# A one-core hybrid decoder layer: the issue order of all five queues written out by a list scheduler in the source, with fixed numbers of PSUM banks

## Chip, cores and metric

The kernel runs on one core of a Trainium2 chip. The metric is the device time of one execution in microseconds (us), from runs that are not profiled in detail, as a median; a profiled execution beside them gives the views that are read here. Engines: PE is TensorE (PEld its weight loads), DVE is VectorE, ACT is ScalarE, POOL is GpSimd, SP is SyncE, which here only issues DMAs.

## Reference, cut to what matters

One decoder layer on 512 tokens of width 1024, all in fp32:

```python
h = rms_norm(x, pre_g);  proj = h @ w_in          # columns for four head groups and a gate z
o_moba = moba_attention(mq, mk, mv)               # 8 heads x 64; at 512 tokens it is causal attention
o_nsa  = nsa_attention(nq, compressed, selected, window branches, gates)   # 8 heads x 64, 2 kv heads
o_ret  = retention(rq, rk, rv)                    # 4 heads, key 64, value 128, group norm
o_mem  = memory_attention(cq, mem_k, mem_v)       # 4 heads x 128 over 256 memory tokens
y = (concat(o_moba, o_nsa, o_ret, o_mem) * silu(z)) @ w_out
out = x + rms_norm(y, post_g)
```

## The kernel before

**Numbers.** Each fp32 operand is split into a high and a low part of type fp32r (H is a rounded copy, L is the rest), and a product is three matmuls (H·H, H·L, L·H), accumulated in one PSUM bank. The split costs an ACT cast and a subtraction on POOL or DVE for every operand. Weights come in pieces of 128x1024 (512 KB): one DMA on SP into a ring of two raw tiles (`wr`), the ACT cast of L312, the POOL subtraction of L315 into a ring of four (`w`), in `split_to`. All matmuls go through the helper `mm`, line L213; all ring and weight DMAs through `dma`, line L192.

**Two streams.** `g_stream` runs the projections (`dim_job`, `tok_job`: two banks or one of tag G), the norm of the memory, the gates z, and at the end the output projection (`out_job`). `a_stream` runs 28 attention units of four score tiles each (16 NSA, 8 MoBA, 4 memory heads) and then retention (`ret_stream`). The main loop takes a step of one or the other by the ratio of PE time so far (`RATIO`), and that is the program order.

**A unit.** A score tile i: two or three matmuls into a bank S; mask (L961), maximum (L963), reciprocal and gate factor (L921, L923) on DVE; exp (L964) and scaling (L926) on ACT; a 32x32 transpose on DVE into `tb` (L895). When all four are done, `tb` goes by one DMA to DRAM (`pd`) and comes back by four DMAs (`pf`), which completes the transposition. ACT casts it (L914), POOL subtracts (L917), and the tiles `pt` feed the PV matmuls into a bank U (`bU<-pt`). A head's U is emptied by an ACT copy (L987) and a DVE addition (L991). Steps follow each other at lags of one to three score tiles (`LAGS`).

**What sets the order.** The source gives a program order; the compiler's scheduler simulates the machine with its own cost model and orders each engine's queue, with 'keep in program order' edges on some instructions only (`PIN = "hp"`: the first loads, the casts H of L914, the first PV matmul of each step; and nearly all of the start-up, through `pin`). On the chip each queue is executed strictly in that order. PSUM has 8 banks of 128x512 fp32. Tags had up to 5 (S), 2 (T, transposes), 2 (U), 3 (G) and 2 (start-up) buffers, more than 8 in all: the compiler gives out the banks as its schedule has them free.

Of the kernel before, what the change touches and what calls it, by code (L numbers as in the profile page):

```python
# [17 lines left out]
F32 = mybir.dt.float32  # L18
# [6 lines left out]
S = 512  # L25
# [137 lines left out]
LAST_BANK = "U"  # L163
# [6 lines left out]
RATIO = (3.7, 4.39, 2.78, 1.7)  # L170


def hybrid_kernel(ctx, tc, io):
# [100 lines left out]

    def pin(i):

        tc.keep_in_program_order(i)

    state = {"load": 0, "split": 0}

# [515 lines left out]
    def y_evac(t, src, a, b, k):  # L796

        junk = t_([128, 512], F32, "P", PB)
        ACT.activation(junk[:, :b - a], src, AF.Square, accum_out=ssy[:, t, k:k + 1])
        DVE.tensor_tensor(ys[t][:, a:b], src, pg[0][:, a:b], op=ALU.mult)  # L800

    def mean_part(t, ks):

# [4 lines left out]
    def finish(t, k, parts):  # L808
        ACT.activation(ssy[:, t, 3:4], ssy[:, t, k:k + 1], AF.Sqrt, bias=ssy[:, t, 0:1], scale=1.0 / D)
        DVE.reciprocal(ssy[:, t, 3:4], ssy[:, t, 3:4])  # L810
        for a, b in parts:
            y, x = ys[t][:, a:b], xres[t][:, a:b]
            DVE.scalar_tensor_tensor(y, y, ssy[:, t, 3:4], x, op0=ALU.mult, op1=ALU.add)
            nc.sync.dma_start(io["out"][128 * t:128 * t + 128, a:b], y)

    def out_prepare():
        ids = yield from grab(7)
        p = slot(ids[0], [128, 1024], F32)
        nc.sync.dma_start(p, io["post_g"].to_broadcast([128, 1024]))
        pg.append(p)  # L820
        for t in range(4):
            xr = ring("pf", FB, [128, 4, 10, 32], F32).rearrange("p i b c -> p (i b c)")[:, :1024] if t < 2 else slot(ids[3 + t], [128, 1024], F32)
            nc.sync.dma_start(xr, io["x"][128 * t:128 * t + 128, :])
            xres.append(xr)
            ys.append(slot(ids[1 + t], [128, 1024], F32))

# [60 lines left out]
    class Turned:  # L887
# [22 lines left out]
        def split(u, i):  # L910
            n, b = u.blocks(i), u.base(i)
            src = u.near[:, :, b:b + n, :].rearrange("p i k c -> p k i c")
            H, L = [x.rearrange("p k (i c) -> p k i c", i=4) for x in u.place(i)]
            h = ACT.copy(H, src)  # L914
            if "h" in PIN:
                tc.keep_in_program_order(h)
# [11 lines left out]
    class Unit(Turned):  # L928
# [39 lines left out]
        def pv(u, kt):  # L968
            if kt == 0 and u.first:
                u.U[0] = bank("U")  # L970
            U = u.U[0]
            v = vtiles[u.v]
            n = 512 - 128 * kt
            c = 2 * cost(n)
            lastmm = u.last and kt == 3
            for a, pt in enumerate((u.ptH, u.ptL)):
                i = mm(U[:, 128 * kt:512], v[:, u.vh, kt, :], pt[:, 4 * kt:4 * kt + 4 - kt, :],
                   u.first and kt == 0 and a == 0, lastmm and a == 1 and u.cmp_head is None)
                if a == 0 and "p" in PIN:
                    tc.keep_in_program_order(i)  # L980
            if lastmm:
                if u.cmp_head is not None:
                    g = u.cmp_head // 4
                    mm(U, vcz[0][:, u.cmp_head, :], ptc[g][0][:, u.cmp_head % 4 // 2, :], False, True)
                    c += 216
                tmp = t_([64, 512], F32, "P", PB)
                ACT.copy(tmp, U[64:128, :])  # L987
                if u.out not in o_tiles:
                    o_tiles[u.out] = t_([128, 512], F32, "o", 2)
                o = o_tiles[u.out]  # L990
                DVE.tensor_tensor(o[64 * u.half:64 * u.half + 64, :], U[0:64, :], tmp, op=ALU.add)  # L991
                if u.frees:
                    free.extend(u.frees())
            return c
# [6 lines left out]
    class MemUnit(Turned):  # L1001
# [30 lines left out]
        def pv(u, m):  # L1032
# [2 lines left out]
            c = slice(128 * u.h, 128 * u.h + 128)  # L1035
            i = mm(u.U, mv[m][:, 0, c], u.ptH[:, m, :], m == 0, False)
            if "p" in PIN:
                tc.keep_in_program_order(i)
# [380 lines left out]
    plan("NKVC")  # L1419
    plan("NQ0", "CMPK")  # L1420
    plan("NKQ0", "CMPV")
    nc.scalar.dma_start(grow[0].bitcast(F32), io["pre_g"])
    nc.scalar.dma_start(first, io["first"])
# [4 lines left out]
    for t in range(4):  # L1428
# [3 lines left out]
        xx.append(xt)  # L1432
        if t < 2:
            load_to(t)
    nc.sync.dma_start(small, io["small"])
    nc.sync.dma_start(consts, io["consts"])
    mraw = [free.pop(0), free.pop(0)]
    split_to(1)
    wps = bank("S")
# [56 lines left out]
    while streams:  # L1496
# [59 lines left out]
```

## Time and profile before

| what | value |
| --- | --- |
| device time, median of 3 runs | 529.08 us (525.64 to 533.41) |
| the profiled execution's own time | 527.68 us |
| its span, first to last instruction | 525.9 us |
| instructions | 8817 |
| busy: PE, ACT, DVE, POOL | 97%, 68%, 61%, 60% of the span |
| mean granted TensorE clock | 0.992 of 2.4 GHz |

Work outside the span is 527.68 - 525.9 = 1.8 us. A busy PE is not a PE at its peak: a matmul's end is modelled, and the next one overlaps it, so the rate is read from start to start. A wait shorter than that overlap does not show as idle time.

### The profile page before, as it was taken

How to read it: one execution, taken by the hardware profiler on the slowest of the kernel's cores; microseconds unless marked ns; L12 is line 12 of the kernel's file. 1: busy time of each engine (PE TensorE's matmuls, PEld its weight loads, DVE VectorE, ACT ScalarE, POOL GpSimd, SP SyncE). 2: the span in 40 equal slices, each digit the busy share in tenths (PEclk: the TensorE clock that was granted, in tenths of full speed). 3: DMA queues.
4: the chain of work that ended last, by engine and by line, in shares of the span. 5: the costliest groups of instructions: out<-in, count | busy, mean ns of one | idle time of the engine just before them, and what ended most of it. 6: DMA issues, size and time to landing. Idle time of an engine off the chain costs nothing.

```text
span 525.9 us, 8817 instructions
## 1 busy us (share of the span) xinstructions
PE 511.2 (97%) x2854; PEld 444.0 (84%) x2854; DVE 321.7 (61%) x973; ACT 359.9 (68%) x807; POOL 317.5 (60%) x232
## 2 busy tenths in 40 slices
PE   8999999999999999999979999999999999999995
PEld 5988788878888988898858898999899888888884
DVE  6629268766888957757785756359746254652006
ACT  6567689667977889779897977658686474423202
POOL 3165755655876495956766688675566798352600
PEclk9999999999999999999988999999999999999999
DMA  8432437866786795755868868857464464231304
GB/s 309 170 116 95 152 120 219 272 211 221 262 248 227 248 294 164 247 176 176 284 180 251 251 205 288 260 166 248 156 208 154 161 199 129 112 121 43 118 0 160
DMA packets 42335, 100.16 MB, mean 190 GB/s; under 512 B 4529, under 2 KB 21681, under 8 KB 42290
## 3 DMA queue, kind: packets, MB, share of 16 engines
q1 hardware_dynamic: 42144, 99.53, 58.9%
q8 instruction: 22, 0.36, 0.3%
q14 instruction: 23, 0.19, 0.1%
q10 hardware_dynamic: 146, 0.08, 0.1%
HBM read 73.38 MB, written 26.21 MB: 189 GB/s over the span
## 4 chain that ended last, share of the span: by engine, by line
PE 57%; DMA 15%; ACT 12%; POOL 5%; DVE 4%; issue 4%; SPq 2%; ACTq 0%; DVEq 0%; POOLq 0%
PE bG L213 32%; PE bU L213 11%; PE bS L213 10%; DMA pd<-tb 4%; DMA wr<-in_w 4%; POOL w L315 4%; DMA pf<-pd 4%; PE bT L213 3%; ACT w L312 3%; ACT bS L964 2%; SPq L192 2%; ACT pt L914 1%; DMA zd<-R 1%; ACT R L452 1%; ACT bS L926 1%
## 5 line engine op out<-in xcount | busy, mean ns | idle before, releaser
L315 POOL TENSOR_TENSOR w<-wr,w 128x1024 fp32r<-128x1024 f32 x76 | 182.9, 2413 | 99.9 <-ACT w L312 88.5
L213 PE MATMUL bG<-hH,w 128*128 128x512 f32 x576 | 189.8, 397 | 0.2 <-POOL w L315 0.2
L917 POOL TENSOR_TENSOR pt<-pf,pt 128x128 fp32r<-128x128 f32 (+2 forms) x112 | 93.0, 857 | 64.3 <-ACT pt L914 60.0
L213 PEld LDWEIGHTS bG<-hH,w 128*128 128x128 f32 x576 | 108.3, 190 | 22.5 <-POOL w L315 0.8
L213 PE MATMUL bG<-hL,w 128*128 128x512 f32 x288 | 113.5, 394 | 0.0
L312 ACT CAST w<-wr 128x1024 fp32r<-128x1024 f32 x76 | 79.5, 1050 | 49.0 <-DMA wr<-in_w 21.3
L213 PE MATMUL bG<-w,hH 128*128 128x256 f32 (+1 forms) x416 | 82.4, 293 | 0.5 <-DVE R L450 0.4
L213 PEld LDWEIGHTS bG<-w,hH 128*128 128x128 f32 x416 | 66.5, 190 | 2.8 <-PE bG L213 0.9
L895 DVE STREAM_TRANSPOSE tb<-bS 128x128 f32<-128x128 f32 (+2 forms) x112 | 55.4, 500 | 21.9 <-ACT bS L926 21.4
L213 PE MATMUL bS<-R,R 128*128 128x256 f32 (+4 forms) x280 | 61.5, 318 | 2.3 <-DVE tb L895 2.3
L213 PEld LDWEIGHTS bG<-hL,w 128*128 128x128 f32 x288 | 54.6, 190 | 10.2
L213 PE MATMUL bG<-w,hL 128*128 128x256 f32 (+1 forms) x208 | 59.9, 291 | 0.0
L213 PE MATMUL bU<-pt,R 128*128 128x512 f32 (+3 forms) x264 | 56.2, 331 | 3.1 <-DVE o L991 1.2
L914 ACT CAST pt<-pf 128x128 fp32r<-128x128 f32 (+2 forms) x112 | 44.5, 456 | 21.4 <-DMA pf<-pd 18.2
L926 ACT ACTIVATE bS<-bS,st 128x128 f32<-128x128 f32 (+2 forms) x112 | 53.7, 497 | 5.8 <-DVE st L925 2.6
L213 PEld LDWEIGHTS bU<-pt,R 128*128 128x128 f32 x264 | 45.9, 192 | 9.9 <-ACT pt L914 2.5
L213 PEld LDWEIGHTS bS<-R,R 128*128 128x128 f32 x280 | 44.8, 189 | 8.1 <-DVE tb L895 3.0
L964 ACT ACTIVATE bS<-bS,st 128x256 f32<-128x256 f32 (+2 forms) x72 | 40.1, 557 | 10.8 <-DVE st L963 9.2
L213 PEld LDWEIGHTS bG<-w,hL 128*128 128x128 f32 x208 | 39.4, 190 | 0.8
L963 DVE TENSOR_REDUCE st<-bS 128x1 f32<-128x256 f32 (+2 forms) x72 | 38.4, 545 | 0.5
L921 DVE RECIPROCAL st<-st 128x1 f32<-128x1 f32 x112 | 16.6, 154 | 19.3 <-ACT bS L964 16.4
L213 PE MATMUL bG<-w,R 128*128 128x256 f32 (+1 forms) x144 | 24.5, 320 | 0.0
(199 smaller groups left out, 776.6 us busy)
## 6 DMA issues: line engine op xcount, KB each, us to landing
wr<-in_w SPq DMA_DIRECT2D x76, 512.0 KB, 3.7
pd<-tb SPq DMA_DIRECT2D x24, 640.0 KB, 3.6
pf<-pd SPq DMA_DIRECT2D x96, 160.0 KB, 3.6
zd<-R SPq DMA_DIRECT2D x8, 512.0 KB, 4.7
R<-in_mem SPq DMA_DIRECT2D x4, 512.0 KB, 6.4
zb<-zd SPq DMA_DIRECT2D x8, 256.0 KB, 3.7
od<-zb SPq DMA_DIRECT2D x8, 256.0 KB, 4.1
R<-zd SPq DMA_DIRECT2D x4, 512.0 KB, 4.1
```

The source lines that it names most:

```text
L192: i = nc.sync.dma_start(out, a)
L213: return PE.matmul(out, a, b, start=first, stop=last)
L312: h = ACT.copy(H[:, c], w[:, c])
L315: eng.tensor_tensor(L[:, c], w[:, c], H[:, c].bitcast(F32), op=ALU.subtract)
L452: ACT.copy(ks[a][rows[1 - a]], ks[a][rows[a]].bitcast(F32))
L895: DVE.transpose(u.tb[:, :, b:b + n, :].rearrange("p j k c -> p k j c"), p[:, :128 * n].rearrange("p (k j c) -> p k j c", k=n, j=4))
L914: h = ACT.copy(H, src)
L917: POOL.tensor_tensor(L, src, H.bitcast(F32), op=ALU.subtract)
L921: DVE.reciprocal(st[:, 2:3], st[:, 1:2])
L926: ACT.activation(s[:, :w], s[:, :w], AF.Copy, scale=st[:, 2:3])
L963: DVE.tensor_reduce(st[:, 0:1], p[:, :w], axis=AX.X, op=ALU.max, negate=True)
L964: ACT.activation(s[:, :w], p[:, :w], AF.Exp, bias=st[:, 0:1], accum_out=st[:, 1:2])
```

## The change

Every engine call goes through a wrapper (`Engine`) that records the instruction in an `Order`. At the end of the kernel `order.run()` plays the recorded instructions through five in-order queues and one DMA queue with durations and latencies fitted as formulas (`RATES`, `DMA_ISSUE`, `WAIT`), and `order.fix()` chains each engine's instructions in the order that came out, with edges that set the order of issue and add no wait. PE and SP take, of what is ready within 60 ns of the earliest (`PATIENCE`), the first in program order; ACT, DVE and POOL take the one with the earliest due time, worked back from the PE's program order. The other order edges go (`PIN = ""`); the start-up's pins stay, as edges in the recorder. A tile's first write waits for the use of the tile `bufs` before it with its tag, so banks are dealt in program order: S has 4 and now also takes the transposes, U has 1, G has 3. The start-up's two banks are taken from tag U. One DVE multiplication at the very end is pinned. No arithmetic, shape or transfer changes.

```diff
-PS_BUFS = {"S": 5, "T": 2, "U": 2, "G": 3}
-BANKS = {"S": "S", "T": "T", "U": "U", "G": "G", "C": "S"}
+PATIENCE = 60
+DUE = {"PE": 0, "ACT": 1, "DVE": 1, "POOL": 1, "SP": 0}
+DUE_LAG = 300
+WAIT = 45
+DMA_ISSUE = 352
+PS_BUFS = {"S": 4, "U": 1, "G": 3}
+BANKS = {"S": "S", "T": "S", "U": "U", "G": "G", "C": "S"}
-PIN = "hp"
+PIN = ""
...
+class Order:
+    RATES = {"ACT": (170, 0.87), "DVE": (175, 1.02), "POOL": (200, 2.16)}
...
+    def touch(self, op, ap, write):
...
+        inst["w" if write else "r"].append((op["id"], p0, p1, mask))
+        inst["ops"].add(op["id"])
+        if write and inst["old"] is not None:
+            op["pre"] |= inst["old"]["ops"]
+        if inst["prev"] is not None:
+            op["hold"].add(inst["prev"])
+
+    def record(self, name, fn, i, args, kw):
...
+        if "dma" in fn:
+            kb = math.prod(tuple(outs[0].shape)) / 256
+            far = outs[0].space == bass.MemoryType.DRAM
+            small = tuple(outs[0].shape)[0] == 32
+            op["cost"], op["dma"] = DMA_ISSUE, 870 if small else (930 if kb > 200 else 250) + kb * (1.32 if far else 1.47)
+        elif name == "PE":
+            n = math.prod(tuple(outs[0].shape)[1:])
+            op["cost"] = max(108.5, 11 + 0.4246 * n)
+            op["lag"] = op["cost"] + 180
+        else:
+            a, b = self.RATES[name]
+            if fn == "reciprocal" and n > 16:
+                b = 6.3
+            if name == "DVE" and n < 32:
+                a = 140
+            op["lag"] = a + b * n + (190 if kw.get("accum_out") is not None else 0)
+            op["cost"] = op["lag"] - (60 if name == "POOL" else 103 if n >= 32 else 75)
...
+        op["lead"] = op["cost"] + DUE_LAG + (1660 + op["dma"] if "dma" in op else 0)
...
+    def pin(self, i):
+        op = next(o for o in reversed(self.ops) if o["i"] is i)
+        op["hold"] |= {op["prev"]} - {None}
+        return i
+    def run(self):
...
+        due, t = [0.0] * len(ops), 0.0
+        for o in ops:
+            if o["eng"] == "PE":
+                due[o["id"]] = t
+                t += o["cost"]
+            else:
+                due[o["id"]] = math.inf
+        for o in reversed(ops):
+            k = o["id"]
+            for j in after[k]:
+                due[k] = min(due[k], due[j] - (1.0 if k not in ops[j]["pre"] else o["lead"]))
...
+        free = {e: 700.0 for e in avail}
+        line, queue, end = {e: [] for e in avail}, 0.0, 0.0
+        for _ in ops:
+            best = None
+            for e, a in avail.items():
+                if not a:
+                    continue
+                t = max(free[e], min(ready[k] for k in a))
+                k = min((due[k] if DUE[e] else 0, k) for k in a if ready[k] <= t + PATIENCE)[1]
+                t = max(t, ready[k])
+                if best is None or t < best[0]:
+                    best = (t, e, k)
+            t, e, k = best
+            o = ops[k]
+            avail[e].remove(k)
+            line[e].append(k)
+            free[e] = done = t + o["cost"]
+            if "dma" in o:
+                queue = max(queue, done + 1290) + o["dma"]
+                o["fin"] = done = queue + 370
+            else:
+                done = t + o.get("lag", o["cost"])
+            o["t"] = t
+            end = max(end, done)
+            for j in after[k]:
+                p = ops[j]
+                if k not in p["pre"]:
+                    at = t
+                elif p["eng"] == e == "PE":
+                    at = free[e]
+                else:
+                    at = done + WAIT
+                ready[j] = max(ready[j], at)
+                left[j] -= 1
+                if not left[j]:
+                    avail[p["eng"]].append(j)
+        return line, end
+
+    def fix(self):
+        line, end = self.run()
+        for ids in line.values():
+            for a, b in zip(ids, ids[1:]):
+                self.tc.add_manual_dep(self.ops[b]["i"].ins, self.ops[a]["i"].ins.name, mybir.DependencyInfo(
+                    mybir.DependencyClass.NoSync, mybir.DependencyReason.DATA), reason="order of issue")
+        return end
+
...
-    PE, ACT, DVE, POOL = nc.tensor, nc.scalar, nc.vector, nc.gpsimd
+    order = Order(tc)
+    PE, ACT, DVE, POOL, SP = [order.engine(e, n) for e, n in (
+        (nc.tensor, "PE"), (nc.scalar, "ACT"), (nc.vector, "DVE"), (nc.gpsimd, "POOL"), (nc.sync, "SP"))]
...
-        i = nc.sync.dma_start(out, a)
+        i = SP.dma_start(out, a)
         if kind in PIN:
-            tc.keep_in_program_order(i)
+            order.pin(i)
...
-        tc.keep_in_program_order(i)
+        order.pin(i)
...
+        i = DVE.tensor_tensor(ys[t][:, a:b], src, pg[0][:, a:b], op=ALU.mult)
+        if k == 2:
+            pin(i)
...
-    preg = [psum.tile([128, 512], F32, name="bP", tag="bP", bufs=2) for _ in range(2)]
+    preg = [bank("U") for _ in range(2)]
...
+    order.fix()
```

## Rows read from the trace of the kernel before

**Rows 1.** The page, busy time of each engine (us, share, instructions).
```profile
PE 511.2 (97%) x2854; PEld 444.0 (84%) x2854; DVE 321.7 (61%) x973; ACT 359.9 (68%) x807; POOL 317.5 (60%) x232
```
**Rows 2.** Groups of PE by shape, the largest: busy us, mean ns, idle before.
```profile
L213 PE MATMUL bG<-hH,w 128*128 128x512 f32 x576 | 189.8, 397 | 0.2 <-POOL w L315 0.2
```
**Rows 3.** The chain that ended last: start us, us, what.
```profile
283.78 1.22 PE bU L213 x8
...
302.45 3.88 PE bG L213 x32
...
486.12 2.75 PE bS L213 x12
```
**Rows 4.** Timeline of PE, at the start: start us, us, instruction.
```profile
1.43 2.07 PE L213 MATMUL bS<-P 128*128 128x512 f32 x4 [1.43 <-POOL P L1427]
...
6.98 1.97 PE L1394 MATMUL bT<-keep,x 128*128 128x128 f32 x8
```
**Rows 5.** Timeline of PE, the last matmuls.
```profile
518.04 1.58 PE L213 MATMUL bU<-w,R 128*128 128x256 f32 x12
```
**Rows 6.** Windows: us, busy us (instructions) by engine, clock, DMA share, GB/s.
```profile
262.00:282.00 20.00, 16.52 (x66) 12.96 (x65) 14.67 (x46) 18.12 (x43) 12.65 (x12) 0.83 0.68 205
...
340.00:395.00 55.00, 52.97 (x408) 50.72 (x408) 36.94 (x138) 39.22 (x96) 33.94 (x31) 1.00 0.63 197
```
**Rows 7.** Timeline of PE, 266 to 280 us.
```profile
266.70 0.60 PE L383 MATMUL bT<-keep,R 128*128 128x128 f32 x4
268.40 1.07 PE L213 MATMUL bS<-R,R 128*128 128x256 f32 x4 [1.09 <-DVE tb L895]
270.69 0.73 PE L213 MATMUL bS<-R,R 128*128 128x512 f32 x2 [1.23 <-DVE tb L895]
272.59 2.61 PE L213 MATMUL bU<-pt,R 128*128 128x512 f32 x8 [1.17 <-DVE o L991]
275.00 0.73 PE L213 MATMUL bG<-hH,w 128*128 128x512 f32 x1
...
279.42 0.61 PE L213 MATMUL bG<-hH,w 128*128 128x512 f32 x2
```
**Rows 8.** Timeline of POOL in the same stretch: the last weight piece before the stall.
```profile
263.01 2.39 POOL L315 TENSOR_TENSOR w<-wr,w 128x1024 fp32r<-128x1024 f32 x1
```
**Rows 9.** Timeline of PE, two of the waits between 340 and 395 us.
```profile
347.83 0.50 PE L213 MATMUL bU<-pt,R 128*128 128x512 f32 x1 [0.70 <-ACT pt L914]
...
371.62 1.42 PE L213 MATMUL bU<-pt,R 128*128 128x512 f32 x5 [0.39 <-POOL pt L917]
```
**Rows 10.** Waits of all engines: us in total, times, longest.
```profile
ACT pt L914 <- DMA pf<-pd: 18.2, 9, 4.4
```
**Rows 11.** Waits of the DMA queue.
```profile
SPq L192 <- POOL w L315: 167.7, 56, 11.8
```
**Rows 12.** The tile pf: time from issue to landing.
```profile
DMA to landing us min/median/max: 2.5/3.5/7.5
```
**Rows 13.** The tile bU: who empties it, durations min/median/max.
```profile
L987 ACT COPY P<-bU x16: 578/584/586, 126.6 to 352.7; 64x512 f32<-64x512 f32 x16
L991 DVE TENSOR_TENSOR o<-bU,P x16: 666/683/685, 127.5 to 353.4; 64x512 f32<-64x512 f32 x16
```
**Rows 14.** The page's costliest groups: the steps that hold a bank S.
```profile
L895 DVE STREAM_TRANSPOSE tb<-bS 128x128 f32<-128x128 f32 (+2 forms) x112 | 55.4, 500 | 21.9 <-ACT bS L926 21.4
...
L926 ACT ACTIVATE bS<-bS,st 128x128 f32<-128x128 f32 (+2 forms) x112 | 53.7, 497 | 5.8 <-DVE st L925 2.6
...
L964 ACT ACTIVATE bS<-bS,st 128x256 f32<-128x256 f32 (+2 forms) x72 | 40.1, 557 | 10.8 <-DVE st L963 9.2
...
L963 DVE TENSOR_REDUCE st<-bS 128x1 f32<-128x256 f32 (+2 forms) x72 | 38.4, 545 | 0.5
```
**Rows 15.** Timeline of ACT, the last of six table loads.
```profile
429.91 1.28 ACT L1163 ACT_TABLE_LOAD   x1
431.34 0.66 ACT L1163 ACTIVATE bS<-bS,keep 128x512 f32<-128x512 f32 x1
```

More of the change, by code (lines that the diff above doesn't have):

```diff
@@ L170, with __init__, engine, region @@
 RATIO = (3.7, 4.39, 2.78, 1.7)
+class Order:
+    RATES = {"ACT": (170, 0.87), "DVE": (175, 1.02), "POOL": (200, 2.16)}
+    def __init__(self, tc):
+        self.tc, self.ops, self.seen, self.tags = tc, [], {}, {}
+        self.last = {}
+    def engine(self, eng, name):
+        return Engine(self, eng, name)
+    @staticmethod
+    def region(ap):
+        dims = [tuple(d) for d in ap.ap]
+        if ap.space == bass.MemoryType.DRAM:
+            return 0, 1, -1
+        step, parts = dims[0]
+        p0, c0 = divmod(ap.offset, step) if step else (0, ap.offset)
+        mask = (1 << 1 + sum(st * (n - 1) for st, n in dims[1:])) - 1
+        return p0, p0 + parts, mask << c0
+    def touch(self, op, ap, write):
+        t = ap.tensor
+        if not hasattr(t, "tag"):
+            return
+        if t.name not in self.seen:
+            inst = self.seen[t.name] = {"r": [], "w": [], "ops": set(), "old": None, "prev": None}
+            line = self.tags.setdefault(t.tag, [])
+            bufs = t.tag_meta.bufs
+            if len(line) >= bufs:
+                inst["old"] = line[len(line) - bufs]
+            if line and line[-1]["ops"]:
+                inst["prev"] = min(line[-1]["ops"])
+            line.append(inst)
+        inst = self.seen[t.name]
+        p0, p1, mask = self.region(ap)
+        near = t.tag.startswith("b")
+        for k in ("w", "r") if write or near else ("w",):
+            for o, a, b, m in inst[k]:
+                if near or a < p1 and p0 < b and m & mask:
+                    op["pre"].add(o)
+        inst["w" if write else "r"].append((op["id"], p0, p1, mask))
[5 more added lines that the diff above has]
+    def record(self, name, fn, i, args, kw):
+        outs = [args[0]] + [kw[k] for k in ("accum_out",) if kw.get(k) is not None]
+        ins = [x for x in list(args[1:]) + [v for k, v in kw.items() if k not in ("accum_out",)] if hasattr(x, "tensor")]
+        op = {"id": len(self.ops), "eng": name, "i": i, "pre": set(), "hold": set()}
+        n = max(math.prod(tuple(x.shape)[1:]) for x in outs + ins)
+        if "dma" in fn:
[15 more added lines that the diff above has]
+            op["cost"] = op["lag"] - (60 if name == "POOL" else 103 if n >= 32 else 75)
+        for x in ins:
+            self.touch(op, x, False)
+        for x in outs:
+            self.touch(op, x, True)
+        op["lead"] = op["cost"] + DUE_LAG + (1660 + op["dma"] if "dma" in op else 0)
+        op["pre"].discard(op["id"])
+        op["prev"] = self.last.get(name)
+        self.last[name] = op["id"]
+        self.ops.append(op)
+    def pin(self, i):
[3 more added lines that the diff above has]
+    def run(self):
+        ops = self.ops
+        left = [len(o["pre"] | o["hold"]) for o in ops]
+        after = [[] for _ in ops]
+        for o in ops:
+            for p in o["pre"] | o["hold"]:
+                after[p].append(o["id"])
+        ready = [0.0] * len(ops)
+        due, t = [0.0] * len(ops), 0.0
+        for o in ops:
+            if o["eng"] == "PE":
[7 more added lines that the diff above has]
+                due[k] = min(due[k], due[j] - (1.0 if k not in ops[j]["pre"] else o["lead"]))
+        avail = {e: [] for e in ("PE", "ACT", "DVE", "POOL", "SP")}
+        for o in ops:
+            if not left[o["id"]]:
+                avail[o["eng"]].append(o["id"])
+        free = {e: 700.0 for e in avail}
[42 more added lines that the diff above has]
+        return end
@@ L979, in pv @@
                 if a == 0 and "p" in PIN:
-                    tc.keep_in_program_order(i)
+                    order.pin(i)
             if lastmm:
@@ L1037, in pv @@
             if "p" in PIN:
-                tc.keep_in_program_order(i)
+                order.pin(i)
             mm(u.U, mv[m][:, 0, c], u.ptL[:, m, :], False, False)
@@ L1421, in hybrid_kernel @@
     plan("NKQ0", "CMPV")
-    nc.scalar.dma_start(grow[0].bitcast(F32), io["pre_g"])
-    nc.scalar.dma_start(first, io["first"])
+    ACT.dma_start(grow[0].bitcast(F32), io["pre_g"])
+    ACT.dma_start(first, io["first"])
     pin(ACT.activation(ssy[:, 0, 0:1], eps, AF.Sqrt))
```

23 lines of the change are left out of this document (16 added, 7 removed).

## The prediction

> **What bounds the kernel now.** I read the page first: PE is busy 97% of the span, the next engine (ACT) 68% [rows 1]. So the kernel is bound by PE, and all that an order of issue can give is the time in which PE does not issue at its own rate. That rate I take from start to start in the chain of waits, where PE runs through: 12 matmuls of 512 columns in 2.75 us are 0.229 us each, 32 of 256 in 3.88 us are 0.121, and eight PV matmuls of one score tile group, two each of 512, 384, 256 and 128 columns, take 1.22 us, of which 0.70 is for the 512s and 256s [rows 3], so that 384 and 128 columns are near 0.17 and 0.09. The list of PE's groups by shape (its largest row is [rows 2]) adds up to 1367 matmuls of 512, 1084 of 256, 116 of 384 (at 0.175), 96 of 280 (taken at 0.13) and 191 of 128 or fewer (at 0.11, to be on the safe side): 313.0 + 131.2 + 20.3 + 12.5 + 21.0 = 498.0 us. PE begins at 1.4 us [rows 4]; its last matmul ends at 518.04 + 1.58 = 519.6 [rows 5], and 6.3 us of evacuation, norm and store follow to the end of the span. The floor of this work is 498.0 + 1.4 + 6.3 = 505.7 us. The span is 525.9: PE loses 20.2 us.
>
> Then I ask where. (a) Start: the 11 matmuls before 6.98 us take 5.55 us where 11 x 0.229 = 2.5 [rows 4]: 3.0 lost. (b) One hole: the windows show 262 to 282 us with 16.5 of 20 us busy and a granted clock of 0.83, where the later stretch has 1.00 [rows 6]. In the timeline of PE it lies between 266.70 and 279.42: 4 transposes (0.44), 4 + 2 score matmuls (0.6 + 0.46), 8 of PV (1.22) and 11 of projection (2.5) are 5.2 us of work in 12.7: 7.5 lost [rows 7]. 3.5 of it are the three waits 1.09, 1.23 and 1.17. Most of the rest is the clock, which was at its upper level (2.4 GHz) before them and fell to the lower one behind them: projection matmuls then start about 0.43 us apart, until 279. (c) 340 to 395 us: 55 - 52.97 = 2.0 us idle [rows 6], waits for `pt` or for an operand beside it, 0.4 to 0.7 us each [rows 9]. (d) The remaining 20.2 - 3.0 - 7.5 - 2.0 = 7.7 us are bits, most too short to show as idle.
>
> **What the change does to each.** It adds no instruction, byte or semaphore of its own; chained edges on one engine cost nothing when that engine issues in order anyway. It only moves.
>
> *Order of PE.* (b) is a fault of order. Behind the waiting score matmuls stood projection matmuls, which start at 275.00 with no wait of their own [rows 7]; POOL had finished the last weight piece before the hole at 263.01 + 2.39 = 265.4 [rows 8]. The old schedule believed the scores' inputs (`tb` transposed, banks S and U emptied) to be early; DVE, the releaser, was late. A scheduler that uses durations near the measured ones puts G matmuls there: a piece holds 24 of 512 columns, 5.5 us, more than the 3.5 us of waits, and without the idle the clock does not fall. Gain between 0 and 7.5; I take 7.5, because the cover was there in this very stretch. (c) is alike: the PV matmul at 347.83 waits for an ACT cast behind a landing that came late, and projections run directly after it. Gain 0 to 2.0; I take 2.0.
>
> *The bits (d).* A new order can remove them or make others. The new one has no more slack: PE takes a score or PV matmul as soon as it is due in the plan, and every deviation of the chip is paid there. Some 112 score and 112 PV steps cross from another engine to PE; 7.7 us are 0.034 us each now. Bounds: all 7.7 gained, or the bits tripled (0.1 each, 15 more). I take 3 gained: durations nearer to the trace make these misses smaller, but not zero.
>
> *Start and tail.* Nearly all of the start is pinned in both, and the last 6.3 us are one chain; 0, between -1 and +1.
>
> *DMAs.* The `p`, `h` and PV pins go, so every DMA on SP, cast of L914 and first PV matmul may move past others. SP waits 167.7 us in total for POOL to free a raw weight tile, up to 11.8 us at once [rows 11], with the `pd` and `pf` transfers queued behind; a new order changes who stands behind whom. The plan gives landings by formula, 3 to 5 us; a `pf` landing took 2.5 to 7.5 us, median 3.5 [rows 12]. If one is late, ACT stands at L914 with exp, scalings and weight casts behind it: that happened 9 times for 18.2 us [rows 10], and PE lost little of it (0.70 us behind the longest [rows 9]), since projections covered it. Price 0 here, as long as projections are ready; the rival below takes the cover away.
>
> *PSUM.* U falls from 2 buffers to 1: a new head's first PV waits for the ACT copy and the DVE addition of the last, 0.58 + 0.68 = 1.26 us, 16 times [rows 13]. Nothing if projections fill it, 16 x 1.26 = 20 us if never. I take 0: a head ends every 15 us (226 us from the first to the last, over 15), and projections run all that time. S falls to 4 and takes the transposes too: a score tile's bank is busy some 0.545 + 0.557 + 0.497 + 0.500 = 2.1 us on DVE and ACT [rows 14]; the 24 units of these heads have 96 tiles in some 226 + 15 us, one every 2.5 us, so four banks leave each tile 10 us. I take 0, at most a bit of (d).
>
> *Tables.* ACT loads a function table six times, 1.28 us each, and the exponential, root and silu runs lie apart [rows 15]. The new plan does not price these loads, and roots that wait for no one (the memory's norm) could fall among exponentials: two to four more loads, 2.6 to 5.1 us of ACT. ACT is busy 68% of the span [rows 1], so I put 0 on the path. The Trainium skill (ScalarE: Activation LUTs, section 'What ACT_TABLE_LOAD costs') speaks against this change more sharply: each switch also drains the engine, about 2.7 us in all. The trace doesn't agree: the activation starts 0.15 us after the load [rows 15]. By the page's figure four more would be, as an estimate, 11 us of ACT, and the sum the same, as ACT has 166 us idle.
>
> **Sum.** 527.68 - 7.5 - 2.0 - 3.0 = 515.2 us for an execution like the profiled one (span 513.4, 1.8 around it). That execution lies 1.4 us under the median of 529.08; the forecast is 0.974 of the median, 2.6% faster. A measurement of this kernel tells about 2% from no change: under 518.5 is faster, over 539.7 slower.
>
> **Rivals.**
> 1. *The fixed order gives back what it gains.* The hole is gone, but a plan without slack pays at every joint: 224 joints at 0.034 + 0.04 us are 9 us more, or another hole with its fall of the clock appears elsewhere (7.5). 527.7 - 9.5 + 7.5 to 9 = 526 to 527, within 2%. For it: the bits exist already, under a schedule that was also planned without slack. Against: their size, and that no second hole exists in the old order. To this group belong smaller gains, down to 519 (only b gained, and ACT tables or bits give back a little). Chance 0.36.
> 2. *Late landings jam ACT, slower.* Place: ACT at L914, 28 units. The old order stood there 9 times, 2.0 us on average, and the longest (4.4 us [rows 10]) cost PE 0.70 us at 347.83 [rows 9]. If the new order casts each unit at the planned landing, with PV planned right behind and no projection left between, 28 x 0.70 = 20 us, and two falls of the clock at 7.5 - 3.5 = 4 us each: 515.2 + 28 = 543. It decides from 539.7 - 515.2 = 24.5 us, 0.87 us of PE a unit with the clock's part, which asks for landings some 1 us behind the formula on average. For it: the spread of 2.5 to 7.5 [rows 12]. Against: one wait in three units before, and PE hardly waits for anything now. The single bank U, uncovered in half of its 16 turns (10 us), adds to it. Chance 0.11.
> 3. *It does not do what it says:* the plan's banks are not the compiler's. Three tiles of tag U are in use at once at the output projection (two for it, one for retention), so a bank's real owner can differ from the plan's, and a wait appears that the plan doesn't have. From 395 us on projections alone cover it; a few us, 518 to 525, in rival 1's band. Chance inside it.
>
> **Numbers.** Forecast with its own range, 507 to 518.5 (floor 505.7 + 1.8 = 507.5): 0.53. Rival 1 with 3: 0.36. Rival 2: 0.11. So faster 0.53, same 0.36, slower 0.11. The range goes from 507 to 531: it takes in all of the forecast's and nearly all of rival 1's cases; what is left outside, some 0.17, lies nearly all above (rival 2, and a PSUM bank uncovered in part).
>
> **What would show it.** Right: no window with a clock below 0.99; PE's idle time outside the start and the tail under 2 us in all, against 3.5 + 2.0 in (b) and (c) alone now; ACT, DVE and POOL busy times unchanged within 1 us; six table loads; span 511 to 516. The weight of projections moves into the places where `pt` is awaited, so waits at L914 may grow without PE noticing. Rival 1: PE without long waits, but its mean step from start to start above 0.229 and 0.121. Rival 2: ACT's wait for `pf` at over 20 places, and PE waiting for ACT at L914. Wrong altogether: more instructions on any engine, more matmuls or another count of DMAs.

## The result, and the profile after

The changed kernel takes 531.33 us (median of 4 runs, 530.56 to 535.2), the kernel before beside it on the same chip 527.36. The ratio is 1.0111, 95% interval 1.0065 to 1.0156: about 1% slower, within the 2% that count as no change, and just outside the range of the forecast (507 to 531). The profiled execution takes 531.85 us with a span of 530.1; before it was 527.68 and 525.9.

The page of the changed kernel, busy time by engine, and the row of the granted clock over 40 slices (they answer to [rows 1]):

```profile
PE 511.7 (97%) x2854; PEld 439.4 (83%) x2854; DVE 325.7 (61%) x973; ACT 363.5 (69%) x807; POOL 318.7 (60%) x232
...
PEclk9999999999999999999999999999999999999999
```

No work was added: instruction counts of PE, DVE, ACT and POOL are those of before, and so is, within 0.5 us, PE's busy time, 511.7 against 511.2 us. (The program as a whole has 8834 instructions instead of 8817, 17 semaphore instructions more; e14 below, which has the chained edges alone, has 8817, so they come with the new order and not with the edges.) ACT and DVE are 3.6 and 4.0 us busier, which no one waits for as such. So of the 4.2 us more of span 3.7 are idle PE. Where, the windows say. After (us, busy us and instructions of PE, PEld, DVE, ACT, POOL; clock, DMA share, GB/s; the third and fifth answer to [rows 6]):

```profile
20.00:215.00 195.00, 191.10 (x985) 160.62 (x985) 134.16 (x419) 149.97 (x332) 119.27 (x82) 1.00 0.62 195
215.00:262.00 47.00, 45.47 (x263) 39.47 (x262) 35.67 (x120) 40.13 (x101) 32.02 (x25) 1.00 0.74 226
262.00:282.00 20.00, 19.26 (x96) 15.24 (x95) 15.71 (x50) 19.72 (x47) 13.86 (x13) 1.00 0.84 248
282.00:340.00 58.00, 56.99 (x349) 50.26 (x348) 35.86 (x110) 46.22 (x105) 44.55 (x33) 1.00 0.77 239
340.00:395.00 55.00, 53.17 (x418) 51.50 (x417) 39.40 (x141) 42.95 (x101) 35.38 (x27) 1.00 0.65 197
395.00:470.00 75.00, 73.78 (x384) 62.13 (x383) 39.85 (x78) 37.27 (x69) 50.59 (x37) 1.00 0.43 146
```

and four windows of before that were not shown yet:

```profile
20.00:215.00 195.00, 194.75 (x1012) 166.04 (x1012) 137.19 (x433) 151.66 (x342) 123.95 (x84) 1.00 0.63 201
215.00:262.00 47.00, 46.65 (x267) 40.90 (x266) 33.02 (x113) 38.94 (x95) 31.06 (x26) 1.00 0.70 218
...
282.00:340.00 58.00, 58.00 (x370) 52.76 (x368) 35.28 (x109) 46.84 (x106) 44.38 (x34) 1.00 0.79 252
...
395.00:470.00 75.00, 75.00 (x393) 64.31 (x392) 37.19 (x78) 38.22 (x69) 50.89 (x31) 1.00 0.44 145
```

The hole of before is gone, as forecast: from 262 to 282 us PE issues 96 matmuls where it issued 66 [rows 6], the clock is 1.00 instead of 0.83, and the idle time is 0.74 instead of 3.48 us. But idle time has come up nearly everywhere else: 195 - 191.10 = 3.90 us from 20 to 215 (before 0.25), 1.53 from 215 to 262 (0.35), 1.01 from 282 to 340 (0), 1.22 from 395 to 470 (0). From 340 to 395 it is 1.83 (2.03). The sum of the six windows is 10.23 us, before 6.11: 4.1 more, nearly the whole difference of the spans.

What PE waits for, the list of its waits (us in total, times, longest):

```profile
PE bS L347 <- DVE st L347: 3.3, 4, 1.4
PE bU L347 <- ACT pt L347: 2.4, 4, 1.4
PE bS L347 <- POOL w L347: 1.8, 2, 1.5
```

These are single waits, at most 1.4 to 1.5 us long, at the joints between engines. Before, outside the start and the hole, none was longer than 0.7 us:

```profile
PE bU L213 <- ACT pt L914: 1.1, 2, 0.7
```

One of the long ones in the timeline of all engines (start us, us, instruction, and the idle time before it with its releaser):

```profile
248.90 0.66 ACT L347 ACTIVATE bS<-bS,st 128x512 f32<-128x512 f32 x1
...
249.47 0.60 ACT L347 CAST pt<-pf 128x256 fp32r<-128x256 f32 x2
249.59 0.72 DVE L347 STREAM_TRANSPOSE tb<-bS 128x512 f32<-128x512 f32 x1 [0.89 <-ACT bS L347]
...
252.15 0.39 PE L347 MATMUL bG<-hL,w 128*128 128x512 f32 x1
...
252.68 0.55 ACT L347 ACTIVATE bS<-bS,st 128x384 f32<-128x384 f32 x1
...
253.08 0.67 DVE L347 TENSOR_TENSOR o<-bU,P 64x512 f32<-64x512 f32 x1
253.14 0.20 ACT L347 ACTIVATION_READ_ACCUMULATOR bS<-bS,st 128x1 f32 x1
...
253.68 0.14 DVE L347 RECIPROCAL st<-st 128x1 f32<-128x1 f32 x1
...
253.87 0.19 PEld L347 LDWEIGHTS bS<-R,R 128*128 128x128 f32 x1 [1.75 <-ACT bS L347]
...
253.90 0.36 PE L347 MATMUL bS<-R,R 128*128 128x256 f32 x1 [1.36 <-DVE st L347]
...
254.09 0.61 PE L347 MATMUL bG<-hH,w 128*128 128x512 f32 x2
```

The score matmul of 253.90 and its weight load of 253.87 wait for ACT and for DVE. The ACT step that ended last before the weight load was over at 253.34 (253.14 + 0.20), so the last release came from DVE: its steps of 253.08 and 253.68 end at 253.75 and 253.82. (Whether the matmul waited for a bank or for an operand, these rows don't tell.) Projections that wait for nothing of their own stand right behind it in PE's queue (254.09). On ACT nothing is late through one cause: from 248.90 to 253.90 it runs with no idle time that the profile shows. The matmul's place in the queue asks for DVE and ACT to be done sooner than they are.

Two rows that stand beside [rows 10] and [rows 11], the waits of ACT for a landing and of the DMA queue for POOL:

```profile
ACT pt L347 <- DMA pf<-pd: 5.4, 5, 1.8
```

```profile
SPq L347 <- POOL w L347: 198.2, 62, 8.4
```

ACT now waits for a `pf` landing 5 times for 5.4 us in all, where it was 9 times and 18.2. The DMA queue waits longer than before, 198.2 us, but no wait in PE's list names a DMA.

### The profile page after: what moved, and what is told of

Same layout as the page of the kernel before. It is cut to its first block, busy times and chain, and to the rows that moved or that the text cites. A ratio compares the mean times of both kernels' runs of the same rounds, so it can differ in the third digit from the quotient of the medians.

```text
span 530.1 us, 8834 instructions
## 1 busy us (share of the span) xinstructions
PE 511.7 (97%) x2854; PEld 439.4 (83%) x2854; DVE 325.7 (61%) x973; ACT 363.5 (69%) x807; POOL 318.7 (60%) x232
## 5 line engine op out<-in xcount | busy, mean ns | idle before, releaser
L347 PE MATMUL bG<-hH,w 128*128 128x512 f32 x576 | 195.0, 393 | 0.0
L347 POOL TENSOR_TENSOR pt<-pf,pt 128x256 fp32r<-128x256 f32 (+2 forms) x112 | 94.3, 855 | 47.8 <-ACT pt L347 44.8
L347 ACT ACTIVATE bS<-bS,st 128x256 f32<-128x256 f32 (+3 forms) x200 | 99.7, 514 | 23.6 <-DVE st L347 22.2
L347 PE MATMUL bS<-R,R 128*128 128x256 f32 (+4 forms) x280 | 62.7, 319 | 4.0 <-DVE st L347 1.7
L347 PE MATMUL bU<-pt,R 128*128 128x512 f32 (+3 forms) x264 | 59.8, 330 | 2.4 <-ACT pt L347 2.4
L347 PEld LDWEIGHTS bU<-pt,R 128*128 128x128 f32 x264 | 44.5, 188 | 11.9 <-ACT pt L347 4.1
L347 ACT CAST pt<-pf 128x256 fp32r<-128x256 f32 (+2 forms) x112 | 47.7, 453 | 5.7 <-DMA pf<-pd 5.4
L347 DVE TENSOR_REDUCE st<-bS 128x1 f32<-128x256 f32 (+2 forms) x88 | 45.1, 523 | 1.3 <-PE bS L347 0.5
L347 DVE TENSOR_TENSOR R<-bG,R 128x128 fp32r<-128x128 f32 (+4 forms) x62 | 23.3, 390 | 34.8 <-ACT R L347 23.9
L347 DVE TENSOR_TENSOR bS<-bS,keep 128x128 f32<-128x128 f32 x88 | 24.7, 290 | 19.2 <-PE bS L347 18.7
```

Source lines behind the costliest of these rows:

```text
L347: i = f(*args, **kw)
```

## The experiments

Fifteen kernels ran. Each ratio is to runs of the kernel before on the same chip (its median there was 525.6 us beside e1 to e4, 526.6 beside e5 to e8, 524.8 beside e9 to e12, 526.3 beside e13 to e15).

| run | us | ratio (95%) |
| --- | --- | --- |
| the change | 531.33 | 1.0111 (1.0065 to 1.0156) |
| e4 old scheduler, new banks | 545.15 | 1.0368 (1.0312 to 1.0425) |
| e5 old scheduler, only U cut | 528.03 | 1.0028 (1.0000 to 1.0056) |
| e6 old scheduler, only S and T cut | 545.37 | 1.0351 (1.0300 to 1.0402) |
| e7 list order planned with the old banks | 547.17 | 1.0405 (1.0373 to 1.0436) |
| e13 the change's order, old banks | 530.39 | 1.0079 (1.0052 to 1.0107) |
| e14 the old order, chained | 526.01 | 0.9999 (0.9963 to 1.0034) |
| e1 durations | 529.09 | 1.0071 (1.0045 to 1.0098) |
| e2 WAIT 0 | 543.47 | 1.0351 (1.0282 to 1.0420) |
| e3 WAIT 200 | 531.94 | 1.0139 (1.0087 to 1.0191) |
| e9 WAIT 70 | 527.98 | 1.0069 (1.0046 to 1.0092) |
| e8 durations and WAIT 70 | 523.47 | 0.9964 (0.9940 to 0.9987) |
| e10 e8 with the old pins | 524.40 | 0.9972 (0.9938 to 1.0006) |
| e11 patience 30, WAIT 55 | 524.77 | 1.0005 (0.9984 to 1.0027) |
| e12 patience 90, WAIT 85 | 526.46 | 1.0022 (0.9994 to 1.0050) |
| e15 patience 30, WAIT 65, old pins | 522.07 | 0.9916 (0.9885 to 0.9947) |

### Do the banks cost, or the order?

**e4: the banks alone.** In the kernel before:

```diff
-PS_BUFS = {"S": 5, "T": 2, "U": 2, "G": 3}
-BANKS = {"S": "S", "T": "T", "U": "U", "G": "G", "C": "S"}
+PS_BUFS = {"S": 4, "U": 1, "G": 3}
+BANKS = {"S": "S", "T": "S", "U": "U", "G": "G", "C": "S"}
```

with the two start tiles taken from U.

> The kernel before, with its compiler's order and its pins, but with the changed kernel's banks (S 4 with the transposes, U 1, G 3, the start-up's two from U). Theory D: the loss is in the order alone, 527 +- 3. Rival B: the banks alone cost what the change cost or more, 531 and up.

545.15 us, 3.7% slower: more than the whole change costs. The compiler's scheduler, given these banks, makes a kernel that is worse than the changed one by 14 us.

**e5 and e6: one tag each.** e5 cuts U alone (and takes the start tiles from it), e6 lets only S and T share four banks:

```diff
-PS_BUFS = {"S": 5, "T": 2, "U": 2, "G": 3}
+PS_BUFS = {"S": 5, "T": 2, "U": 1, "G": 3}
```

```diff
-PS_BUFS = {"S": 5, "T": 2, "U": 2, "G": 3}
-BANKS = {"S": "S", "T": "T", "U": "U", "G": "G", "C": "S"}
+PS_BUFS = {"S": 4, "U": 2, "G": 3}
+BANKS = {"S": "S", "T": "S", "U": "U", "G": "G", "C": "S"}
```

> The kernel before (its own order of issue), with one part of the change alone: tag U holds one bank instead of two, and the two start tiles bP come from it. Both parts together cost 19 us on top of 525.6. If the single bank U is what costs, because a head's first PV matmul waits for the copy and the addition of the head before (1.26 us by rows 13, 16 times, 20 us if nothing covers it), this runs at 538 to 545 and PE shows waits at the first PV matmul of a head. If the score and transpose banks are what costs, it stays within 525 to 530.

> The kernel before, with the other part alone: scores and transposes share one tag of four banks instead of having five and two of their own; U stays at two. If the shared four banks are what costs (a transpose now takes a bank that a score tile would have had, and the holes at 287 and 303 us of the run with both parts start there), 538 to 545 with holes near those places. If the single bank U costs, 525 to 530. If only both together jam, this and the run with U alone each stay under 532.

U is nearly free: 1.5 us, interval 0 to 3. Nearly all of the loss is S and T. The profile of e6 shows where. The window of the damage:

```profile
282.00:320.00 38.00, 27.47 (x143) 23.82 (x143) 23.74 (x77) 29.11 (x71) 22.97 (x22) 0.78 0.56 177
```

10.5 us idle, and the clock at 0.78. Timeline of PE and then of ACT in it:

```profile
296.29 0.60 PE L383 MATMUL bS<-keep,R 128*128 128x128 f32 x4
301.65 0.80 PE L213 MATMUL bG<-R,w 128*128 128x256 f32 x2 [4.77 <-ACT R L330]
```

```profile
298.96 1.53 ACT L914 CAST pt<-pf 128x128 fp32r<-128x128 f32 x4 [4.50 <-DMA pf<-pd]
300.52 0.58 ACT L987 COPY P<-bU 64x512 f32<-64x512 f32 x1
301.13 0.84 ACT L330 ACTIVATE R<-bS,keep 128x256 fp32r<-128x256 f32 x2
```

PE stands 4.77 us for an ACT cast, and that cast stands behind the casts of L914, for which ACT waited 4.50 us for a landing. In the list of waits that wait has grown to

```profile
ACT pt L914 <- DMA pf<-pd: 30.1, 13, 4.5
```

against [rows 10]. This is the mechanism of the forecast's second rival, a late landing that jams ACT with PE's next operand behind it; it occurred, but in the old scheduler with the new banks, not in the changed kernel. How the four shared banks bring the scheduler to an order with this jam is not shown.

**e7: the list order, planned with the old banks.** In the changed kernel the two lines of e4's diff the other way round; the plan counts the same twelve banks as the program.

> The changed kernel with the banks of before: S 5, T 2, U 2, G 3 in the plan and in the program, list order kept. The chip has eight banks and these tags add up to twelve, so which tile waits for which is again the compiler's to deal. Theory 'the order gains and the banks cost, and the two add up': 531.3 - 19 = 512, at most 518. Theory 'the order is only good if the plan knows the banks it will get': the plan counts on four banks more than there are, PE stands for banks that it took to be free, 533 to 545, with the waits at bank tiles as the largest.

547.17 us, 4.1% slower, the dearest of all and 2 us over the upper expectation. The largest row in the list of PE's waits, and then a wait of PE in the timeline of all engines:

```profile
PE bS L347 <- DVE R L347: 4.4, 4, 1.7
```

```profile
253.79 0.72 DVE L347 STREAM_TRANSPOSE tb<-bS 128x512 f32<-128x512 f32 x1 [0.89 <-ACT bS L347]
...
254.56 0.50 PE L347 MATMUL bG<-hH,w 128*128 128x512 f32 x1 [1.19 <-DVE tb L347]
```

At 254.56 PE starts a tile of G that has waited 1.19 us for DVE to transpose a tile of S out (it ends at 254.51). A projection (`bG<-hH,w`) reads neither `tb` nor bS, so it waited for the bank, which the plan took to be free. The tags of e7 add up to twelve banks, those of the change to eight. The Trainium skill (PSUM — Partial Sum Buffer, section 'PSUM: the matmul accumulator') gives PSUM eight banks; this wait agrees, in that G got a bank of S. That bank waits are the largest, as expected, is not shown: in the largest row the R that DVE wrote can also be an operand of the score matmul.

**e13: the changed kernel's order, old banks.** e7 left open whether it was the banks or the order made for them. Here the plan keeps counting 4, 1 and 3, so that every engine's order is that of the changed kernel, while the tiles ask for the old numbers:

```diff
-PS_BUFS = {"S": 4, "U": 1, "G": 3}
-BANKS = {"S": "S", "T": "S", "U": "U", "G": "G", "C": "S"}
+PS_BUFS = {"S": 5, "T": 2, "U": 2, "G": 3}
+BANKS = {"S": "S", "T": "T", "U": "U", "G": "G", "C": "S"}
...
-            line = self.tags.setdefault(t.tag, [])
-            bufs = t.tag_meta.bufs
+            tag = t.tag.replace("bT_", "bS_")
+            line = self.tags.setdefault(tag, [])
+            bufs = {"bS_": 4, "bU_": 1, "bG_": 3}.get(tag[:3], t.tag_meta.bufs)
```

> The changed kernel with exactly its own order on every engine (the plan still counts S 4, U 1, G 3), but the tiles ask for the old banks, S 5, T 2, U 2, G 3, so that the dealing of the eight banks is not static any more. Theory 'the static banks cost by themselves': PE's waits at bank tiles shrink, 520 to 527. Theory 'banks cost only through the order that is made for them; the loss of 4 us is the order's': 529 to 533, as the changed kernel.

530.39 us. The intervals of e13 and of the change overlap widely, and PE's first long window is the same, 191.32 busy against 191.10:

```profile
20.00:215.00 195.00, 191.32 (x987) 161.15 (x987) 134.12 (x420) 150.21 (x333) 119.46 (x82) 1.00 0.63 195
```

So the static banks cost nothing by themselves under this order. e7 and e13 ask for the same banks and differ by 17 us only in what the plan believed when it made the order.

**e14: the old order, chained.** The kernel before, whose own order is written into the source and chained edge by edge as the change does it:

```diff
-        line, end = self.run()
+        line, end = self.given(), 0.0
```

> The kernel before with exactly its old order on every engine and its old banks, but each instruction chained to the one before it on its engine, as the change does it. The control for the edges: if chaining costs nothing, as the forecast took it, it runs with the kernel before, ratio 0.997 to 1.003. If the edges bring semaphores or waits of their own, as the 17 semaphore instructions more in the changed kernel could mean, 1.004 to 1.01.

Ratio 0.9999. The edges cost nothing that the interval of 0.4% either way could show. (The old order under the new banks, the crossing that is missing, was not tried.)

### Do the plan's constants cost?

**e1: durations.** The plan's formula for an ACT operation of n columns is 170 + 0.87 n ns (`RATES`): 281, 504 and 615 ns for 128, 384 and 512. The groups by shape of the changed kernel (busy us, mean ns of one), which mix the exps and the scalings of a score tile, show 342, 556 and 665:

```profile
L347 ACT ACTIVATE bS<-bS,st 128x512 f32<-128x512 f32 x48 | 31.9, 665 | 8.2 <-DVE st L347 7.9
L347 ACT ACTIVATE bS<-bS,st 128x384 f32<-128x384 f32 x48 | 26.7, 556 | 6.0 <-DVE st L347 5.6
...
L347 ACT ACTIVATE bS<-bS,st 128x128 f32<-128x128 f32 x24 | 8.2, 342 | 2.4 <-DVE st L347 2.3
L347 ACT ACT_TABLE_LOAD x6 | 7.7, 1283 | 1.8 <-PEq L1730 1.7
```

and in the timeline above ACT is free again 0.57 us after the `ACTIVATE` of 248.90, where the plan has 615 - 103 = 512 ns. For the scalings, then, 50 to 61 ns were missing. For the exps nothing was, since the plan gives them 190 ns more for their sum: for 384 columns 694 ns, where the exp of 252.68 and the read of its sum take 0.66 us, to 253.34. And the transposes were 7 to 16 ns short: DVE's groups show 312, 443, 576 and 713 ns where the formula (175 + 1.02 n) has 306, 436, 567 and 697. e1 adds more than that, to all of them:

```diff
+            op["lag"] += {"activation": 70, "transpose": 40}.get(fn, 65 if fn == "scalar_tensor_tensor" and n > 32 else 0)
```

> Three durations of the plan are set to what the changed kernel's trace shows back to back: +70 ns on an ACT activation, +40 on a DVE transpose, +65 on a wide scalar_tensor_tensor; banks and everything else stay. Theory D (the plan runs short, so PE is sent to score and PV matmuls before their bank or operand is there): most of the loss behind 28 us goes, 518 to 525 us. Rival B (the four S banks and the one U bank are too few whatever the plan believes): 531 +- 2, as the changed kernel.

529.09 us: 0.4 points better than the change by the ratios, whose intervals overlap, and much less than expected.

**e2, e3 and e9: the time from one engine to the next.** One constant, with 0, 200 and 70 in its place:

```diff
-WAIT = 45
+WAIT = 0
```

> The plan's allowance for a hop between engines goes from 45 to 0 ns; on the chip nothing else changes than the order that follows. Theory D with its second half (no slack in the plan): each hop is now planned too short as well, so PE stands at more joints, 536 to 545 us. Rival B: 531 +- 2.

> The same allowance goes to 200 ns: more than the plan's errors of 40 to 120 ns a step, so PE finds its operands there, but the plan is stretched and fills with other work where it need not. Theory D: 523 to 528 us. Rival B: 531 +- 2, or slower, since banks are held longer in the plan.

> The changed kernel with one constant alone: the plan's time from one engine to the next is 70 ns instead of 45; durations as they were. If the two corrections of e8 add up, this gives e8's gain less that of e1: 531.3 - (7.9 - 2.2) = 525.6, between 524 and 528. If what counts is that the order is right as a whole, so that one wrong term is enough to spoil it, it stays at 529 to 532. A time above 533 would say that the orders scatter by some microseconds for any small change of a constant, and that e8 was in part luck.

543.47, 531.94 and 527.98 us. A plan that is too fast is dear: with 0 the idle time of the first window is 6.7 us and that of the next 4.3.

```profile
20.00:215.00 195.00, 188.34 (x960) 156.70 (x959) 131.98 (x403) 143.58 (x317) 116.31 (x79) 0.99 0.59 189
215.00:262.00 47.00, 42.72 (x248) 37.29 (x247) 32.70 (x99) 39.30 (x90) 28.91 (x23) 1.00 0.63 197
```

One that is too slow is not cheap either: e3 gained nothing, a miss of its expectation. Its PE idles 5.0 us in the first of these windows (189.97 busy), with a clock of 0.98. Why a plan with more time loses there is not shown.

What the time from one engine to the next is can be read in the changed kernel's trace. Timeline of all engines, an ACT cast and the two that wait for it, and then of DVE and of ACT, a step that ACT waits for:

```profile
373.96 0.39 ACT L347 CAST pt<-pf 128x256 fp32r<-128x256 f32 x1
...
374.41 0.50 PE L347 MATMUL bU<-pt,R 128*128 128x512 f32 x1 [1.35 <-ACT pt L347]
374.43 0.75 POOL L347 TENSOR_TENSOR pt<-pf,pt 128x256 fp32r<-128x256 f32 x1 [2.74 <-ACT pt L347]
```

```profile
139.01 0.21 DVE L347 TENSOR_SCALAR st<-st,keep 128x1 f32<-128x1 f32 x1
```

```profile
139.31 0.66 ACT L347 ACTIVATE bS<-bS,st 128x512 f32<-128x512 f32 x1 [0.54 <-DVE st L347]
```

From the end of the one to the start of the other pass 0.06 us to PE, 0.08 to POOL, 0.09 from DVE to ACT, and above, from the `ACTIVATE` of 248.90 to the transpose of 249.59, 0.03. Over all of this trace's waits of more than 0.1 us the medians are 32 ns from ACT to DVE, 35 from DVE to ACT (mostly 94 to 96 where a separate semaphore instruction stands before the step), 53 from ACT to PE and 77 from ACT to POOL. So 45 ns lies in the middle of what these waits show, and 70 above most of them.

**e8: both corrections.** e1's line and `WAIT = 70`.

> The changed kernel with the plan's durations of ACT activations, transposes and wide scalar_tensor_tensor raised to what its trace shows (+70, +40, +65 ns, as in e1) and the plan's time from one engine to the next raised from 45 to 70 ns, between the values that lost by being too short (0: 543.5) and brought nothing by being too long (200: 531.9). Theory 'the plan errs by single durations, so a truer one gives more': 517 to 524, under e1's 529.1. Theory 'no plan without slack can hold, whatever its constants': 527 to 532, like e1.

523.47 us, 0.4% under the kernel before, and the interval leaves 1 out. Each step is clear beside the other one: the hop of 70 ns wins 1.1 points over e1, the durations win 1.05 over e9, both together 1.5 over the change. Alone, each wins 0.4 points, within the noise. That they do more than add up is likely, but only just clear of it: e9's 527.98 us lies at the edge of its 'they add up' (524 to 528).

What e8 does not tell is whether the plan needed truer times or just some room. Its values lie above the rows for the exps, the transposes and most hops, so it gives the plan some slack as well as truer scalings. A plan with exactly the durations of the rows was not run.

### One good draw, or a region? And the pins

e10 is e8 with the pins of before; e11 and e12 keep e1's line and change the constants on either side of e8:

```diff
-PIN = ""
+PIN = "hp"
```

```diff
-PATIENCE = 60
-DUE_LAG = 300
-WAIT = 45
+PATIENCE = 30
+DUE_LAG = 600
+WAIT = 55
```

```diff
-PATIENCE = 60
-WAIT = 45
+PATIENCE = 90
+WAIT = 85
```

> The kernel of e8 (523.5) with the pins of the kernel before put back in the plan: the casts behind a landing, the first PV matmul and the first loads keep the source's order. It tells whether taking the pins away was a gain or a loss of its own. Theory 'the plan does better when it is free': 525 to 530. Theory 'the pins are nearly free, since the plan would put these steps there anyway': 521.5 to 525. Theory 'late landings jam ACT once the pins are gone' (the forecast's second rival): under 521.

> The changed kernel with the durations of e1, 55 ns from engine to engine, patience 30 instead of 60 (how long an engine's choice may wait for a more urgent operation) and the due times 300 ns earlier. It asks whether e8 is one good draw or a region: theory 'region' (any plan with the measured durations and a hop of 55 to 85 ns): 519 to 526, below the kernel before. Theory 'draw': 526 to 533.

> As e11 from the other side: durations of e1, 85 ns from engine to engine, patience 90. The plan's own end is some 3 us later than that of e8, so its order gives up projections' room for slack. Theory 'region': 520 to 527. Theory 'draw': 527 to 533. If it is under e8 in spite of its later plan, slack in the plan is worth more than a short plan.

524.40, 524.77 and 526.46 us: within the expected times each, between 0.3% under and 0.2% over the kernel before. e11 was also expected below the kernel before and is level with it, and e12 is slower than e8, so still more slack is not worth more. Against the change (1.1% over) all three gain. So e8 was no single draw, and the pins that the change takes away are nearly free: e10 and e8 differ by less than their intervals.

**e15: the best of these.** e1's line and

```diff
-PATIENCE = 60
-WAIT = 45
-PIN = ""
+PATIENCE = 30
+WAIT = 65
+PIN = "hp"
```

> The changed kernel with the durations of e1, 65 ns from engine to engine, patience 30, and the pins of before. Theory 'the constants are what was missing': with e8 (523.5) and e10 (524.4) or a little under them, 520 to 524, ratio to the kernel before 0.990 to 0.997. Theory 'e8 was as far as the order can go': 523 to 527.

522.07 us, 0.8% faster than the kernel before (interval 0.5 to 1.2%; clear of the noise, but inside the 2% that count as no change) and 1.9% than the change by the ratios. Its windows:

```profile
20.00:215.00 195.00, 192.72 (x1001) 163.90 (x1002) 135.41 (x430) 150.86 (x339) 122.18 (x83) 1.00 0.63 198
215.00:262.00 47.00, 47.00 (x272) 41.50 (x270) 35.76 (x120) 42.75 (x104) 32.83 (x26) 1.00 0.74 234
262.00:282.00 20.00, 20.00 (x102) 16.62 (x101) 13.95 (x43) 19.24 (x45) 14.69 (x13) 1.00 0.76 235
282.00:340.00 58.00, 57.80 (x385) 53.15 (x384) 35.82 (x112) 46.17 (x106) 45.47 (x34) 1.00 0.79 253
340.00:395.00 55.00, 54.18 (x429) 52.67 (x428) 40.28 (x148) 41.36 (x102) 36.30 (x32) 1.00 0.65 195
395.00:470.00 75.00, 73.68 (x350) 60.87 (x349) 38.26 (x70) 37.51 (x67) 49.96 (x31) 1.00 0.44 141
```

Idle between 215 and 340 us is 0.2 us, where the change had 3.3 and before 3.8; what is left lies in the first window (2.28) and in the last two (0.82 and 1.32).

## Why the prediction was wrong

- **What bounds the kernel** held: PE's work and busy time stayed, and nearly all that was won or lost is time in which PE did not issue.
- **(b), the hole, 7.5 us** was right in kind and nearly in size. Idle went from 3.48 to 0.74 us and the clock stayed up. Counted from start to start against the plan's own formula for a matmul (11 ns and 0.4246 ns a column, at least 108.5; it gives 228 and 120 ns where [rows 3] have 229 and 121), excesses over 5 ns only, the 20 us from 260 lost 7.5 us before and 1.9 after: 5.6 gained. In e15 the same 20 us lost 0.6.
- **(c), 2.0 us** was wrong: 2.03 us idle [rows 6] became 1.83, and by the count above 0.7 us were gained.
- **(d), the bits, "I take 3 gained"** is the step that failed. By the same count all the rest from 20 us on lost 12.5 us before and 21.9 after, (c) among it: 9.4 lost instead of 2.0 + 3 gained. (One profile each; e13, with the same order, lost 19.3, and e14, with the old one, 12.0.) 8.6 of the 9.4 lie in a few places that lost over 150 ns each: 9 before, with 4.2 us together, 20 after, with 12.8. All the smaller ones together stayed at 8.3 and 9.1 us. So what grew is not the bits that the prediction had counted but single waits of up to 1.5 us, in which PE stood before a step of ACT, DVE or POOL that the plan had put earlier.

  The reason given, "durations nearer to the trace make these misses smaller", did not hold. The plan was short at one kind of step that could be seen in the rows of before: the 112 scalings of L926 took 497 ns on average [rows 14]; for their 24, 40, 24 and 24 of 128, 256, 384 and 512 columns the formula gives 440. But most of its other times were near, and near was not enough: e8, which raises them by 25 to 70 ns, also where the rows ask for less, wins 1.5% back. Nor did any plan gain the 3: with e8 and e15 the rest loses 14.7 and 13.6 us, so that e15's gain on the kernel before is all the hole. The bound of 15 us lost held the result; the value taken from between was the wrong one.
- **The sum**: 5.6 gained and 9.4 lost are 3.8 us; the spans differ by 4.2. (The forecast's ratio divides a time built on the profiled execution by the median: 515.2 is 0.974 of 529.08, but 0.976 of its own base of 527.68.)
- **PSUM at 0** holds for the changed kernel: e13 shows that static dealing costs nothing with this order, e5 that U is nearly free under the old scheduler. What it costs to plan for four, one and three banks in the first place, no run shows. But the working behind it, "four banks leave each tile 10 us", was no proof: with the same four banks the old scheduler loses 18.8 us (e6). A mean over 240 us does not see a jam of 20.
- **Rival 1**, "the fixed order gives back what it gains", is what happened, but not the way it was told, "pays at every joint". Its size was missed, 526 to 527 against 531.3 measured: of the 9.5 us of (b) and (c) only 5.6 and 0.7 came. Spread over its 224 joints, 9.4 us are 0.042 each, next to the 0.04 that it took; that is luck, since 20 places carry it. Its sign, "PE without long waits", did not come either.
- **Rival 2** did not happen here, ACT's waits for landings fell to 5.4 us; it is real in e6.
- **Rival 3**, banks that are not the compiler's, is not borne out in the form given (e13 leaves the dealing to the compiler, and the time stays), but it is real in a coarser one: in e7 the plan counts four banks too many, for 20.6 us over the kernel before.
- **The signs**: the clock stayed at 1.00 in the six windows, and there are six table loads. PE's idle time in the six windows is 10.2 us instead of under 2, ACT, DVE and POOL are 3.6, 4.0 and 1.2 us busier instead of within 1, and "no instruction, byte or semaphore of its own" was wrong by 17 semaphore instructions, though not for the edges (e14).
- **Start, DMAs and tables at 0** held: the first 20 us have 17.80 us of PE (before 17.66), the ACT groups above have six table loads of 1283 ns, and chaining is free (e14).

So the change is two halves, each a loss with the other's old state: fewer banks under the old scheduler cost 3.7%, the list order planned with twelve banks 4.1%. Together they are 1.1% slower than before. That rest comes of the plan's times, on an engine and between engines, since raising these alone takes it away and 0.4% more (e8), 0.8% with the pins and a shorter patience (e15). Two things are not settled: whether it is the truer scalings or the slack that helps, and why the plan is so sharp in `WAIT`, where beside the raised durations 45 to 70 gains, while 200 with the old ones does not.

## What to carry to other kernels

An order written out statically needs a plan with some room at each step: with times that were near the trace for most steps it lost 1.1%, 45 ns less a hop cost 12 us more, and 25 to 70 ns more a step turned the loss into a small gain, while a hop of 200 ns gained nothing. So hold the formulas against the rows of the trace first, then try the allowance on both sides. Look for the loss in single waits before spreading it over all joints: here 20 places of some 2850 matmuls carried it. Give the plan every shared resource in the number that it will really get: e7, planned with twelve banks, ran 3.2% behind e13, planned with eight. And test the parts of such a change crosswise: here each half alone looked like a loss of 4%.

## What was not expected

Chaining some five thousand instructions edge by edge left the time where it was (e14, 0.9999), with the instruction counts of [rows 1]:

```profile
PE 511.0 (97%) x2854; PEld 443.8 (85%) x2854; DVE 321.6 (61%) x973; ACT 360.0 (69%) x807; POOL 317.6 (61%) x232
```

And the order reacts out of proportion: 25 ns of `WAIT` are worth 1.1 points beside the raised durations (e1 to e8), and alone 0.4, which is within the noise.
